# Moving weight splits, masks, loads and stores by a step in a two-batch encoder layer

## The chip, the cores and the metric

The kernel runs on one core of one Trainium2 chip. The metric is the device time of one execution in microseconds, as the median of several runs. The engines are TensorE (PE; its weight loads are shown as PEld), VectorE (DVE), ScalarE (ACT), GpSimd (POOL) and SyncE (SP), which only issues transfers here.

## What is computed

One layer of a bidirectional encoder is applied to two batches with shared weights: batch A (`x_prompt`, 1024 tokens) and batch B (`x_sample`, 512 tokens), 1024 channels each, all in fp32.

```python
h = rms_norm(x, pre_w)
cols = h @ w_in          # q|k, v, o, z, gates i and f; attention q, k, v, z; merge gates
y_m = mlstm_mixer(...)   # bidirectional mLSTM, 4 heads x 256, chunks of 128, forward and backward
y_a = dilated_attention(...) * silu(a_z)   # 3 (window, dilation) groups x 8 heads x 64
merged = sigmoid(g0) * (y_m @ w_pm) + sigmoid(g1) * (y_a @ w_pa)
out = merged @ w_out
return x + rms_norm(out, post_w)
```

Inside a chunk the mLSTM weighs the products of q and k with exp(d_log - m), which is zero on one side of the diagonal (on the other side for the backward direction); between chunks it carries a 256 x 256 state and its normaliser. The head's norm and the two gates follow.

## The kernel before

Every fp32 product is made of three matmuls on a pair of halves: `hi`, the operand rounded by a ScalarE copy, and `lo`, the rest by a subtraction on VectorE or GpSimd; `mm3` (line 191) multiplies hi x hi, hi x lo and lo x hi.

The kernel has two parts. The first, up to about 1055 us, makes all projections of batch A, and the value projections of both. The second makes everything else. In the second part TensorE and SP run in the order of the program text (line 1957), while the order on ScalarE, VectorE and GpSimd is chosen when the kernel is built, by a scheduler that models each instruction's time (line 2096). Every engine's queue is worked off in order. `issue_after(x)` orders the instructions of a block behind `x` on the same engine and adds no wait.

The second part is a row of five stages: mLSTM of A (`mlstm`, line 856), attention of A (`attend`, line 1431), mLSTM of B (`mlstm_short`), attention of B, and the rest. Each stage's work is short and full of dependences, so it is filled with dense products, one list for the whole part: the projections of batch B (`short_units`), the output projections of the three blocks of 512 tokens (`branches`, line 1627) and the last product with its norm (`final`, line 1692). A `Fill` object (line 113) hands them out: a unit takes eight steps, one step is the three matmuls of one slice of 128 channels (in `final`, of one slice and 128 tokens), and a stage calls `fill(share)`; `STEPS` and the stage's number of shares say how many steps a share is.

A unit's weights come by a transfer into one of two raw buffers (`load_w`) and are split into one of three pairs of halves (`split_w`, line 245), by ScalarE and VectorE; the very first low half is made on GpSimd. `weights()` (line 138), called by a unit at its first step, calls `load()` (line 124), which splits up to two units' weights at once, until two units are ahead (`ahead`, four from line 2021 on, with five pairs of halves), or as many as buffers are free. The transfer of the next raw weights is asked for behind each split, and issued at the next `tick()`, or at the split that needs it.

`tick()` (line 212) is called once a round. It issues `pace` of the queued loads (`spread(r)` sets the pace such that the queue is empty after `r` rounds) and the stores whose time has come: `put` holds a store back for `lag` rounds. `need(group)` issues what is still missing of a group.

In `mlstm` the rounds go over head, chunk and direction, 64 in all. `rows` loads, for two chunks, the rows of the stabiliser, broadcast to all partitions. `front(k + 1)`, written ahead of `core(k)`, makes the mask `rm` (line 923: an affine_select on GpSimd; line 925: an Exp on ScalarE), multiplies it with the products (line 926), splits the result into `sch` and `scl` (lines 929, 930) and makes the weighted q and k. `core` multiplies by the values into the PSUM tile `num`, of which there are two; line 989 (and 992 for the second half of the chunks) evicts it. `ml_load` (line 830) queues a head's q, k and v; the v tiles' last two columns are set by memsets on GpSimd (lines 846, 849), and head 1 uses other tiles (`V1a`, `V1b`) than head 0. Before the first stage `short_input` (line 651) splits the normalised input of batch B into the tiles `H`, the low halves of the first four slices by GpSimd (line 326); `aside` is the last of these.

In `mlstm_short`, `turn` transposes the normalised output (`hn`, line 1195) on TensorE (line 1202). In `attend` a round makes logits (line 1386), softmax (1398 to 1402), transposes of the weights (1409) and the output (1421), which is evicted at line 1423 into one of ten (A) or six (B) `ot` buffers and stored. `split` (line 1587) is a generator that runs beside dense units, brings rows of `ym` back, and splits them (lines 1604, 1605). `close`, in `final`, squares and sums a product (line 1709), and with the second half of the channels makes the norm and writes the result.

Of the kernel before, what the change touches and what calls it, by code (L numbers as in the profile page):

```python
# [112 lines left out]
class Fill:  # L113
# [3 lines left out]
    def __init__(self, net, units):  # L117
        self.net, self.units, self.gen = net, list(units), None
        self.srcs = [x for u in self.units for x in u.srcs]
        self.raws, self.ready, self.taken, self.base, self.ahead = [], [], 0, 0, 2  # L120
        self.rate = self.due = 0.0
        self.done = 0

    def load(self):

        more = 2
        while (len(self.ready) < min(self.base + len(self.net.wsplit), self.taken + self.ahead, len(self.srcs))
               and (more or len(self.ready) < self.taken)):
            more -= 1
            self.fetch(len(self.ready) + 1)  # L130
            self.ready.append(self.net.split_w(*self.raws[len(self.ready)]))
            self.fetch(len(self.ready) + 1)
# [5 lines left out]
    def weights(self, first=True):  # L138
# [4 lines left out]
        self.load()  # L143
# [11 lines left out]
    def step(self):  # L155
        while self.gen is not None or self.units:
            if self.gen is None:
                self.gen = self.units.pop(0).make(self.weights)
            if next(self.gen, self) is not self:
                self.done += 1  # L160
                return True
# [14 lines left out]
class Net:  # L176
# [653 lines left out]
    def ml_load(self, T, h):  # L830
# [12 lines left out]
        for i, x in enumerate([both[0][:, :1032], both[0][:, 1032:]] if S == BLK else both):  # L843
            x = x.rearrange("p (n c) -> p n c", c=258)
            if i:
                nc.gpsimd.memset(x[:, :, 256:258].bitcast(F32), 0.0)
            else:
                for c in range(2):
                    nc.gpsimd.memset(x[:, :, 256 + c:257 + c].bitcast(F32), 1.0 - 2 * c)
# [6 lines left out]
    def mlstm(self, T, fill, steps, first, banks, lead, after, beside=()):  # L856
# [7 lines left out]
        head, made, turns, rws = {0: first}, {}, {}, {}  # L864
        beside = iter(beside)
        self.lag = 2 if n > 4 else 3
        with ExitStack() as stack:
# [44 lines left out]

            def front(k):
# [5 lines left out]
                uc, wsc, flc = (T.col[:, q, o:o + 1] for q in range(3))  # L919
                rw = rws[h, d, c // 2 * 2][:, c % 2]  # L920
                rm = sb.tile([P, P], F32, name="rm")
                sg = 1 if d == 0 else -1
                nc.gpsimd.affine_select(out=rm, in_=rw[:, 0], pattern=[[sg, P]], compare_op=OP.is_ge, fill=-NEG, base=0,
                                        channel_multiplier=-sg)
                nc.scalar.activation(rm, rm, AF.Exp, scale=-1.0, bias=uc)
# [94 lines left out]
            for _ in prepare(0):  # L1020
                fill(1 / 3)
            front(0)
            coming = None
            for k, (h, i, d) in enumerate(rounds):
# [12 lines left out]
                if k % 4 < 2:  # L1037
                    rows(k // 4 + 1, k % 4)
                if k + 1 < len(rounds):
# [63 lines left out]
    def mlstm_short(self, T, fill, steps, first, banks, lead, after, beside=()):  # L1103
# [11 lines left out]
        with ExitStack() as stack:  # L1115
# [103 lines left out]
            for k, (h, i) in enumerate(rounds):  # L1219
# [20 lines left out]
                self.tick()  # L1240
                turns.pop(k - 1, lambda: None)()
                fill(2 / 3)
# [188 lines left out]
    def attend(self, T, fill, steps, first, banks, outs, after=None, beside=None, at=()):  # L1431
# [4 lines left out]
        self.lag = 3  # L1436
        with ExitStack() as st:
# [26 lines left out]
            for i in range(12):  # L1464
                now = coming
                for j, t in enumerate(now):
                    if j == 1:
                        if i < 11:
                            coming = ready(i + 1)
                            self.spread(T.n - 1 if i else 1)  # L1470
# [116 lines left out]
    def split(self, T, b, row, places, halves):  # L1587
# [5 lines left out]
        got = []  # L1593
        for j, (hi, lo) in enumerate(halves):
            for k in range(5):
                if k < 4:
                    r = row + 4 * j + k
                    t = self.rows_in.pop(0)
                    self.rows_in.append(t)
                    got.append(t)  # L1600
                    self.fetch(("ym", T.S, min(r // 2, 4)), t, T.ym[r, :, b * BLK:(b + 1) * BLK])
                if k:
                    t = got.pop(0)
                    nc.scalar.activation(hi[:, k - 1], t, AF.Copy)
                    nc.gpsimd.tensor_sub(lo[:, k - 1], t, hi[:, k - 1].bitcast(F32))
                yield
# [85 lines left out]
    def final(self, T, b):  # L1692
# [4 lines left out]
        def make(weights):  # L1697
# [8 lines left out]
            def close(u, t, c, p):  # L1706
                r0 = b * BLK + t * P
                o1 = sb.tile([P, BLK], F32, name="mg", bufs=2) if u else o[t]
                nc.scalar.activation(o1, p, AF.Square, accum_out=ss[:, t, u:u + 1])
                if u == 0:  # L1710
                    nc.vector.tensor_mul(o[t], p, pw[:, c])
                    return
                which, xt = xo[t]
                nc.vector.tensor_add(ss[:, t, 4:5], ss[:, t, 0:1], ss[:, t, 1:2])
                nc.gpsimd.tensor_scalar(ss[:, t, 5:6], ss[:, t, 4:5], 1.0 / D, 4 * EPS, op0=OP.mult, op1=OP.add)
# [43 lines left out]
def body(tc, a):  # L1759
# [3 lines left out]
    with ExitStack() as st:  # L1763
# [192 lines left out]
        with ExitStack() as s1:  # L1956
# [36 lines left out]
            with ExitStack() as s2:  # L1993
# [4 lines left out]
                with tc.issue_after(N.aside.ins):  # L1998
                    head = N.ml_load(A, 0)
# [100 lines left out]
```

## Time and profile before

| what | value |
|---|---|
| runs, us | 2284.59, 2285.61, 2280.73 (median 2284.59) |
| the profiled execution, us | 2280.13 |
| its span, us | 2278.3 |
| mean granted TensorE clock | 0.995 |
| PE / PEld busy | 98% / 86% |
| DVE / ACT / POOL busy | 65% / 48% / 27% |
| bytes moved | 425.05 MB, mean 187 GB/s |

The span runs from the first to the last instruction of the program. An engine's busy share is that of its own instructions, without the time in which it waits or issues transfers; the ends of matmuls are modelled. In a timeline a row is: start, duration, engine (with a q: its sequencer, as for transfers), line, operation, out<-in, shape, number, and in brackets the idle time before it and what ended that. In a table of waits the columns are the total, the number and the longest, in us. The granted clock is the share of TensorE's full clock that the throttle let through.

### The profile page before, as it was taken

The numbers are of one execution on the slowest core, as the hardware profiler recorded it, in microseconds if no ns is written. First come the engines' busy times: TensorE is split into PE (matmuls) and PEld (weight loads), VectorE is DVE, ScalarE is ACT, GpSimd is POOL, SyncE is SP. The second block draws the span as 40 slices with busy tenths as digits, with TensorE's granted clock in tenths as the row PEclk, the third lists the DMA queues.
The fourth block names the chain that finished last, engine by engine and source line by source line (L and its number), as shares of the span: only waits on it lengthen the run. The fifth ranks groups of instructions, "written<-read, shape, count | busy, mean of one in ns | idle before, by whom it ended". The sixth has DMA issues, their size and how long they took to land. (4 is left out here: it accounts for less than half of the span.)

```text
span 2278.3 us, 35138 instructions
## 1 busy us (share of the span) xinstructions
PE 2235.8 (98%) x12210; PEld 1950.2 (86%) x12210; DVE 1472.1 (65%) x2789; ACT 1103.1 (48%) x2255; POOL 615.6 (27%) x789
## 2 busy tenths in 40 slices
PE   9999999999999999999999999999999999999998
PEld 9999998888887888887888888989888888888787
DVE  5587556767889655544788775575567744555563
ACT  7444223434444433334777766676644444544432
POOL 1000023333333322222667640001033321411311
PEclk9999999999999999999999999999999999999999
DMA  9545335555323223324766659997777878787673
GB/s 361 188 138 145 112 113 193 197 194 194 126 102 111 93 83 114 136 93 159 250 210 223 159 160 232 237 243 205 207 238 253 258 232 243 207 252 212 225 246 115
DMA packets 253626, 425.05 MB, mean 187 GB/s; under 512 B 26208, under 2 KB 150752, under 8 KB 252680
## 3 DMA queue, kind: packets, MB, share of 16 engines
q1 hardware_dynamic: 249848, 410.20, 57.8%
q10 hardware_dynamic: 3600, 12.59, 1.4%
q8 instruction: 97, 1.59, 0.3%
q14 instruction: 81, 0.66, 0.1%
HBM read 302.72 MB, written 128.37 MB: 189 GB/s over the span
## 5 line engine op out<-in xcount | busy, mean ns | idle before, releaser
L194 PE MATMUL dense<-H,wh 128*128 128x512 f32 x672 | 282.1, 420 | 0.0
L195 PE MATMUL dense<-H,wh 128*128 128x512 f32 x672 | 265.9, 396 | 5.1 <-POOL H L326 5.0
L196 PE MATMUL dense<-H,wl 128*128 128x512 f32 x672 | 266.4, 396 | 0.2 <-DVE wl L253 0.2
L196 PE MATMUL d<-Hh,phla 128*128 128x512 f32 x608 | 236.9, 390 | 1.5 <-DVE phla L538 1.5
L195 PE MATMUL d<-Hl,phla 128*128 128x512 f32 x608 | 236.6, 389 | 0.0
L194 PE MATMUL d<-Hh,phla 128*128 128x512 f32 x608 | 236.5, 389 | 0.0
L195 PE MATMUL d<-vlo,Hh 128*128 128x322 f32 x704 | 219.7, 312 | 0.8 <-DVE vlo L384 0.8
L196 PE MATMUL d<-vhi,Hl 128*128 128x322 f32 x704 | 219.9, 312 | 0.0
L194 PE MATMUL d<-vhi,Hh 128*128 128x322 f32 x704 | 219.8, 312 | 0.0
L253 DVE TENSOR_TENSOR wl<-wraw,wh 128x1024 fp32r<-128x1024 f32 x109 | 139.2, 1277 | 85.3 <-ACT wh L252 83.3
L1398 DVE CUSTOM_DVE_ANT_0 ls<-lg,bias 128x256 f32<-128x256 f32 (+1 forms) x288 | 93.8, 362 | 146.6 <-PE lg L1386 61.7
L194 PE MATMUL d<-Hh,phlb 128*128 128x512 f32 x456 | 177.4, 389 | 0.0
L195 PE MATMUL d<-Hl,phlb 128*128 128x512 f32 x456 | 177.4, 389 | 0.0
L196 PE MATMUL d<-Hh,phlb 128*128 128x512 f32 x456 | 177.4, 389 | 0.0
L556 POOL TENSOR_TENSOR psum_w<-pw_raw 128x512 f32<-128x512 f32 x38 | 57.2, 1506 | 444.3 <-DMA pw_raw<-w_in 432.0
L1402 ACT ACTIVATE ls<-ls,nm 128x256 f32<-128x256 f32 (+1 forms) x288 | 130.5, 455 | 92.7 <-DVE nm L1400 78.7
L252 ACT ACTIVATE wh<-wraw 128x1024 fp32r<-128x1024 f32 x110 | 116.1, 1055 | 88.4 <-PE dense L195 34.4
L196 PEld LDWEIGHTS dense<-H,wl 128*128 128x128 f32 x672 | 127.3, 189 | 29.6 <-DVE wl L253 0.6
L195 PEld LDWEIGHTS dense<-H,wh 128*128 128x128 f32 x672 | 128.3, 191 | 20.8 <-POOL H L326 7.4
L194 PEld LDWEIGHTS dense<-H,wh 128*128 128x128 f32 x672 | 127.7, 190 | 13.6
L196 PEld LDWEIGHTS d<-Hh,phla 128*128 128x128 f32 x608 | 114.1, 188 | 26.4 <-DVE phla L538 2.8
L195 PEld LDWEIGHTS d<-Hl,phla 128*128 128x128 f32 x608 | 114.1, 188 | 23.9
(556 smaller groups left out, 5729.7 us busy)
## 6 DMA issues: line engine op xcount, KB each, us to landing
pw_raw<-w_in SPq DMA_DIRECT2D x76, 512.0 KB
wraw<-w_in SPq DMA_DIRECT2D x76, 512.0 KB
aqk_a<-pwk SPq DMA_DIRECT2D x48, 512.0 KB
aqk_b<-sw SPq DMA_DIRECT2D x48, 256.0 KB
wraw<-w_pm SPq DMA_DIRECT2D x24, 512.0 KB
wraw<-w_out SPq DMA_DIRECT2D x24, 512.0 KB
vb<-w_vp SPq DMA_DIRECT2D x16, 644.0 KB
va<-w_vp SPq DMA_DIRECT2D x14, 644.0 KB
```

The costliest lines, as they stand in the source:

```text
L194: nc.tensor.matmul(out, lh, rh, start=start, stop=False)
L195: nc.tensor.matmul(out, lh, rl, start=False, stop=False)
L196: nc.tensor.matmul(out, ll, rh, start=False, stop=stop)
L252: self.splits = (nc.scalar.activation(hi[:, :n], raw[:, :n], AF.Copy), on.tensor_sub(lo[:, :n], raw[:, :n], hi[:, :n].bitcast(F32)))
L253: on.tensor_sub(lo[:, :n], raw[:, :n], hi[:, :n].bitcast(F32)))
L556: self.nc.gpsimd.tensor_add(s[:, 0], ws[1][:, 0], ws[1][:, 1])
L1398: nc.vector.tensor_tensor_reduce(out=ls[:, hh], in0=ts["lg"][hh], in1=bt[:, hh], scale=1.0, scalar=NEG, op0=OP.add, op1=OP.max, accum_out= ...
L1402: nc.scalar.activation(ls[:, hh], ls[:, hh], AF.Exp, bias=nm[:, hh:hh + 1], accum_out=ot[:, 128 + hh:129 + hh])
```

## The change

- **Weights.** `weights()` splits only what the unit and its successor still lack; all further splits are made by `load()` after the unit's fourth step (`left` counts down). The initial `load()` and `release()` stay.
- **Memsets.** Every memset of the v tiles in `ml_load` is ordered behind `aside`; before, only those of head 0 of batch A were, with the whole call.
- **Masks.** The mask of a round is made by a function of its own, called for round k + 2 ahead of `front(k + 1)`; `rm` gets a third buffer.
- **`mlstm_short`.** `fill(2/3)` stands ahead of `turn` instead of behind it.
- **`attend`.** The loads of the second unit are spread over n - 1 rounds instead of one, and the lag of stores is 2 for batch B instead of 3.
- **`split`.** Rows of `ym` are asked for three steps ahead instead of one, across the two halves, with five buffers instead of three.
- **`close`.** The sum of squares is scaled in the square; the first half's sum gets its epsilon on GpSimd early, so that the addition on VectorE goes.

```diff
-        self.done = 0
+        self.done = self.left = 0
     def load(self):
...
-            self.fetch(len(self.ready) + 1)
-            self.ready.append(self.net.split_w(*self.raws[len(self.ready)]))
-            self.fetch(len(self.ready) + 1)
+            self.split()
+    def split(self):
+        self.fetch(len(self.ready) + 1)
+        self.ready.append(self.net.split_w(*self.raws[len(self.ready)]))
+        self.fetch(len(self.ready) + 1)
     def fetch(self, n):
...
-        self.load()
+        room = min(self.base + len(self.net.wsplit), len(self.srcs))
+        while len(self.ready) < max(self.taken, min(self.taken + 1, room)):
+            self.split()
+        self.left = 4
     def release(self):
...
+                self.left -= 1
+                if self.left == 0:
+                    self.load()
...
-            if i:
-                nc.gpsimd.memset(x[:, :, 256:258].bitcast(F32), 0.0)
-            else:
-                for c in range(2):
-                    nc.gpsimd.memset(x[:, :, 256 + c:257 + c].bitcast(F32), 1.0 - 2 * c)
+            with self.tc.issue_after(self.aside.ins):
+                if i:
+                    nc.gpsimd.memset(x[:, :, 256:258].bitcast(F32), 0.0)
+                else:
+                    for c in range(2):
+                        nc.gpsimd.memset(x[:, :, 256 + c:257 + c].bitcast(F32), 1.0 - 2 * c)
...
-        head, made, turns, rws = {0: first}, {}, {}, {}
+        head, made, turns, rws, masks = {0: first}, {}, {}, {}, {}
...
+            def mask(k):
+                h, i, d = rounds[k]
+                c = i if d == 0 else n - 1 - i
+                o = 32 * d + h * n + c
+                uc = T.col[:, 0, o:o + 1]
+                rw = rws[h, d, c // 2 * 2][:, c % 2]
+                rm = sb.tile([P, P], F32, name="rm", bufs=3)
+                sg = 1 if d == 0 else -1
+                nc.gpsimd.affine_select(out=rm, in_=rw[:, 0], pattern=[[sg, P]], compare_op=OP.is_ge, fill=-NEG, base=0,
+                                        channel_multiplier=-sg)
+                nc.scalar.activation(rm, rm, AF.Exp, scale=-1.0, bias=uc)
+                masks[k] = rw, rm
             def front(k):
-                uc, wsc, flc = (T.col[:, q, o:o + 1] for q in range(3))
-                rw = rws[h, d, c // 2 * 2][:, c % 2]
-                rm = sb.tile([P, P], F32, name="rm")
-                sg = 1 if d == 0 else -1
-                nc.gpsimd.affine_select(out=rm, in_=rw[:, 0], pattern=[[sg, P]], compare_op=OP.is_ge, fill=-NEG, base=0,
-                                        channel_multiplier=-sg)
-                nc.scalar.activation(rm, rm, AF.Exp, scale=-1.0, bias=uc)
+                wsc, flc = (T.col[:, q, o:o + 1] for q in (1, 2))
+                rw, rm = masks.pop(k)
...
+            mask(0)
             front(0)
+            mask(1)
                 self.tick()
...
                     rows(k // 4 + 1, k % 4)
+                if k + 2 < len(rounds):
+                    mask(k + 2)
                     front(k + 1)
...
                 self.tick()
+                fill(2 / 3)
-                fill(2 / 3)
...
-        self.lag = 3
+        self.lag = 3 if T.n > 4 else 2
...
                         if i < 11:
-                            self.spread(T.n - 1 if i else 1)
+                            self.spread(T.n - 1)
...
-        got = []
-        for j, (hi, lo) in enumerate(halves):
-            for k in range(5):
-                if k < 4:
-                    r = row + 4 * j + k
-                    t = self.rows_in.pop(0)
-                    self.rows_in.append(t)
-                    got.append(t)
-                    self.fetch(("ym", T.S, min(r // 2, 4)), t, T.ym[r, :, b * BLK:(b + 1) * BLK])
-                if k:
-                    t = got.pop(0)
-                    nc.scalar.activation(hi[:, k - 1], t, AF.Copy)
-                    nc.gpsimd.tensor_sub(lo[:, k - 1], t, hi[:, k - 1].bitcast(F32))
-                yield
+        got, m = [], 4 * len(halves)
+        for i in range(m + 3):
+            if i < m:
+                t = self.rows_in.pop(0)
+                self.rows_in.append(t)
+                got.append(t)
+                self.fetch(("ym", T.S, min((row + i) // 2, 4)), t, T.ym[row + i, :, b * BLK:(b + 1) * BLK])
+            if i >= 3:
+                t, (hi, lo), k = got.pop(0), halves[(i - 3) // 4], (i - 3) % 4
+                nc.scalar.activation(hi[:, k], t, AF.Copy)
+                nc.gpsimd.tensor_sub(lo[:, k], t, hi[:, k].bitcast(F32))
+            yield
     def along(self, units, make, every):
...
             def close(u, t, c, p):
-                nc.scalar.activation(o1, p, AF.Square, accum_out=ss[:, t, u:u + 1])
+                nc.scalar.activation(o1, p, AF.Square, scale=1.0 / 32, accum_out=ss[:, t, u:u + 1])
+                    nc.gpsimd.tensor_scalar(ss[:, t, 4:5], ss[:, t, 0:1], 4 * EPS, None, op0=OP.add)
                 which, xt = xo[t]
-                nc.vector.tensor_add(ss[:, t, 4:5], ss[:, t, 0:1], ss[:, t, 1:2])
-                nc.gpsimd.tensor_scalar(ss[:, t, 5:6], ss[:, t, 4:5], 1.0 / D, 4 * EPS, op0=OP.mult, op1=OP.add)
+                nc.gpsimd.tensor_scalar(ss[:, t, 5:6], ss[:, t, 1:2], ss[:, t, 4:5], None, op0=OP.add)
...
-                with tc.issue_after(N.aside.ins):
-                    head = N.ml_load(A, 0)
+                head = N.ml_load(A, 0)
...
-            N.rows_in = [N.sraw[:, :BLK]] + [N.osb.tile([P, BLK], F32, name=f"ymr{i}") for i in range(2)]
+            N.rows_in = [N.sraw[:, :BLK]] + [N.osb.tile([P, BLK], F32, name=f"ymr{i}") for i in range(4)]
```

## The prediction

> **What bounds the kernel now.** I read the page first, then a table of busy time by stage, then TensorE's own waits, and at last the timelines of the engines around each long gap.
>
> ```profile
> span 2278.3 us, 35138 instructions
> ...
> PE 2235.8 (98%) x12210; PEld 1950.2 (86%) x12210; DVE 1472.1 (65%) x2789; ACT 1103.1 (48%) x2255; POOL 615.6 (27%) x789
> ```
>
> TensorE is the bound: 2235.8 of 2278.3 us. The change adds and removes no matmul, so all it can return is idle time, 42.5 us, and time at a lowered clock. The profiled execution took 2280.13 us, 1.83 more than its span and 4.5 below the median of 2284.59; I sum against the execution and take the difference from the median. In the stage table the columns are stretch, PE busy, PEld, DVE, ACT, POOL, granted clock, DMA share, GB/s.
>
> ```profile
> 1054.70:1071.00 16.30, 11.24 (x35) 7.42 (x34) 10.89 (x8) 2.97 (x6) 11.99 (x17) 0.79 0.88 300
> 1071.00:1100.00 29.00, 25.96 (x159) 22.02 (x158) 17.22 (x37) 19.60 (x45) 12.00 (x19) 1.00 0.82 287
> 1100.00:1345.00 245.00, 238.32 (x1509) 212.44 (x1508) 194.99 (x423) 179.39 (x452) 171.95 (x289) 0.99 0.60 194
> 1345.00:1385.00 40.00, 34.91 (x204) 29.75 (x203) 21.40 (x65) 20.22 (x55) 3.12 (x12) 0.96 0.72 183
> ...
> 1660.00:1835.00 175.00, 171.13 (x1018) 149.75 (x1017) 128.34 (x308) 76.70 (x145) 55.50 (x89) 1.00 0.80 250
> 1835.00:1900.00 65.00, 60.88 (x315) 51.49 (x314) 29.48 (x65) 31.62 (x72) 19.70 (x18) 0.95 0.88 267
> 1900.00:2130.00 230.00, 228.52 (x1215) 194.49 (x1215) 120.33 (x313) 109.61 (x304) 56.07 (x53) 1.00 0.73 210
> 2130.00:2272.00 142.00, 140.90 (x618) 113.88 (x616) 81.30 (x137) 42.85 (x67) 23.89 (x28) 1.00 0.64 214
> ```
>
> Stretch less PE busy is idle; one less the clock, times the stretch, is what the slow clock costs. Idle plus clock by stage: start of the second half (1054.7 to 1071) 5.1 + 3.4; first mLSTM rounds 3.0; the other rounds 6.7 + 2.4; start of attention A 5.1 + 1.6; short mLSTM 3.9; start of attention B 4.1 + 3.3; its rest 1.5; end 1.1. With the tail behind the last matmul that is most of the idle time, and nothing of the change lies before 1054.7. TensorE's waits (total, times, longest) name what it waits for:
>
> ```profile
> PE num L194 <- ACT X L989: 6.4, 6, 2.3
> PE pt L1409 <- ACT ls L1402: 6.3, 4, 3.7
> PE o L1421 <- ACT ot L1423: 5.5, 3, 2.9
> PE dense L195 <- POOL H L326: 5.0, 2, 4.4
> PE a L1202 <- ACT hn L1195: 2.4, 2, 1.4
> ```
>
> Four of five end on ScalarE, which is only 48% busy: it was blocked in order behind an instruction that waited for something else.
>
> **Start of the second half (V1 memsets behind `aside`, third split later).**
>
> ```profile
> 1042.62 1.06 ACT L252 ACTIVATE wh<-wraw 128x1024 fp32r<-128x1024 f32 x1 [3.34 <-DMA wraw<-w_in]
> 1045.08 4.27 ACT L325 ACTIVATE H<-xs 128x512 fp32r<-128x512 f32 x8
> 1054.79 0.15 POOL L849 MEMSET V1a<- 128x8 f32 x2 [20.41 <-PE d L195]
> 1054.93 2.35 POOL L253 TENSOR_TENSOR wl<-wraw,wh 128x1024 fp32r<-128x1024 f32 x1
> 1057.24 7.30 POOL L326 TENSOR_TENSOR H<-xs,H 128x512 fp32r<-128x512 f32 x4
> 1058.29 6.80 DVE L326 TENSOR_TENSOR H<-xs,H 128x512 fp32r<-128x512 f32 x4
> 1059.54 0.50 PE L195 MATMUL dense<-H,wh 128*128 128x512 f32 x1 [4.36 <-POOL H L326]
> 1070.45 0.39 PE L194 MATMUL dense<-H,wh 128*128 128x512 f32 x1
> 1071.13 0.39 PE L891 MATMUL a<-Q,K 128*128 128x128 f32 x2
> ...
> SPq L231 <- DMA K<-qk_a: 4.2, 2, 2.4
> 1067.03 0.36 SPq L231 DMA_DIRECT2D V0b<-vs_a  x1
> ```
>
> GpSimd's queue is headed by the memset of V1a, whose place the last product of the first half frees only at 1054.79. Behind it stand the first low half (2.35 us) and four pieces of the input (7.30), whose sources ScalarE had written by 1043.7 and from 1045.6 on. With the memsets behind `aside` GpSimd can start at 1043.7 and, at the same durations, ends by 1053.4: before TensorE asks. So the 4.36 us gap goes. VectorE's four pieces, at their old 1.7 us each from about 1057 on, may still hold single steps, but end by 1064, and that matters to nobody, since what is late next is K. The lead of 4 shares is 4 x 210 / 74 = 11 dense steps of 0.68 us (1071.13 less 1070.45), 7.5 us: TensorE is through them at 1062.3 and then needs K, whose second half SP saw land at 1067.03 (it issued V0b on that). So the first product of Q and K comes at 1067.0 instead of 1071.1: 4.1 us gained, but behind a new gap of 4.7 us, and a slow clock after it; the stages with gaps of 3.7 and 2.9 us (the waits above) paid 1.6 and 3.3 for theirs, I take 2.6. Net 1.5. In the first rounds I give back half of the 3.0 us idle, since one wait for a buffer fewer stands before SP's row loads: 1.5. Together 3.0, between -1 (the masks want their rows a round sooner just here, where the transfers are busiest) and 8.
>
> On that clock: the Trainium skill, "TensorE: Matmul & The Clock Gate", Part 1, lets the array fall to half rate only after at least one idle window of about 3.4 us. Here the stage whose longest gap is 2.9 us fell to 0.95, so the trace has it earlier, and the trace decides. By the page's rule the clock in that stage and in the mLSTM rounds would owe nothing to those gaps, and the sum below would be some 5 us smaller.
>
> **mLSTM rounds (masks a round ahead).** Added: one tile; no instruction. Moved: per round one affine_select on GpSimd and one Exp on ScalarE, each ahead of the front of the round before.
>
> ```profile
> 1285.78 1.32 POOL L923 TENSOR_SCALAR_AFFINE_SELECT rm<-rw 128x128 f32<-128x128 f32 x1
> 1287.13 0.40 ACT L925 ACTIVATE rm<-rm,col 128x128 f32<-128x128 f32 x1 [1.98 <-POOL rm L923]
> 1288.44 0.39 PE L194 MATMUL num<-V1a,sch 128*128 128x258 f32 x1 [2.33 <-ACT X L989]
> ...
> L923 POOL TENSOR_SCALAR_AFFINE_SELECT rm<-rw x64: 286/294/1321, 1067.7 to 1330.5; 128x128 f32<-128x128 f32 x64
> ...
>   DMA rw<-rw_a: 10.0, 6
> ...
>   ACT rm L925: 37.6, 38
> ...
> 1083.69 0.42 SPq L231 DMA_DIRECT2D rw<-rw_a  x1
> 1089.49 0.29 POOL L923 TENSOR_SCALAR_AFFINE_SELECT rm<-rw 128x128 f32<-128x128 f32 x1 [2.41 <-DMA rw<-rw_a]
> ```
>
> The longest gap of the rounds is this chain: the mask took 1.32 us instead of its median 0.29, ScalarE waited 1.98 for it, and the eviction L989 that frees `num` stood behind. A mask that was made a round (4.2 us: 262.8 / 63) before cannot hold ScalarE there. This gap and its clock go: 2.3 + 1.6 = 3.9 (the stage's rounded clock says 2.4; 1.6 is what the longer gap of attention A cost). The other 4.4 us of gaps I leave. Against it: ScalarE waited 37.6 us in all for masks, while the stage lost 8.3 us (6.7 + 1.6), 0.22 us per us; the same ratio prices the rows, which now have two rounds (8.4 us) from issue to use instead of three, and needed 5.8 at 1083.69. Behind a mask that waits stand `qw`, `scl` and `ql` on GpSimd, and on ScalarE the evictions. Bounds -4 to 7.
>
> **Weights in the middle of a unit.**
>
> ```profile
> L253 DVE TENSOR_TENSOR wl<-wraw,wh 128x1024 fp32r<-128x1024 f32 x109 | 139.2, 1277 | 85.3 <-ACT wh L252 83.3
> ```
>
> Counts stay; a split of 1.06 us on ScalarE and 1.28 on VectorE moves by four steps. ScalarE no longer waits for the last matmul of the unit before, whose buffer it takes. The weights are still due 12 steps, 8.2 us of pure dense work, after their split. No row gives this a price on TensorE: 0, with the bounds in the 5 us of new gaps below. At the closing projections, where four units are ahead, as many splits fall due per unit as before.
>
> **Start of attention A (`spread`).**
>
> ```profile
> 1368.81 0.33 SPq L210 DMA_DIRECT2D wraw<-w_in  x1
> ...
> 1378.34 1.06 ACT L252 ACTIVATE wh<-wraw 128x1024 fp32r<-128x1024 f32 x1 [8.64 <-DMA wraw<-w_in]
> ```
>
> All loads of the second unit are issued in one round; the raw weights behind them go out at 1368.81 and land at 1378.3, 9.5 us later, with ScalarE standing at their split for 8.64. That makes the 3.7 us wait of the transposes and the slow clock after it, 3.7 + 1.6. Over seven rounds it is two loads a round, as for every later unit. I take 5.3 and allow 3.5 to 6.5.
>
> **Short mLSTM (`fill(2/3)` ahead of `turn`).** Two thirds of a share are 164 / 36 x 2/3 = 3 steps, 2.1 us of cover where the waits were 1.4 and 1.0: 2.4 gone. Without that cover they are back. The transposed result is stored 2 us later, which nobody waits for. Bounds 0 and 2.5.
>
> **Attention B (`lag` 2, rows of `ym` three ahead, `spread`).**
>
> ```profile
> 1873.23 0.63 ACT L1604 ACTIVATE K<-ymr 128x512 fp32r<-128x512 f32 x1 [1.19 <-DMA ymr<-ym_a]
> 1886.61 0.42 DVE L1398 CUSTOM_DVE_ANT_0 ls<-lg,bias 128x256 f32<-128x256 f32 x1 [3.93 <-DMA og_b<-ot]
> ```
>
> VectorE waited 3.93 us for the store of an `ot` buffer, and TensorE's longest wait on an eviction L1423, 2.9 us, came behind it. A round holds six dense steps (290 / 48), 4.1 us, beside its own products, so a store issued one round earlier has landed by then. SP then waits at that store for its eviction L1423, and the loads behind it wait with it, but the eviction is a full round old. The other two of the three waits on L1423 (2.6 of 5.5 us) stand behind ScalarE's waits for a row of `ym`, 1.19 in the one shown; three rows ahead remove them, one at this start and one in the 1.5 us idle after 1900. I take 6.5 of 7.4, and 1.0. Bounds 3 to 9.
>
> **The closing sums.** Twelve VectorE additions leave the chain, twelve GpSimd ones come beside the first half, on an engine that is busy for 24 of 142 us there; the last addition stood on the end of the kernel:
>
> ```profile
> 2272.76 0.16 DVE L1714 TENSOR_TENSOR ss<-ss 128x1 f32<-128x1 f32 x1 [1.65 <-ACT mg L1709]
> ```
>
> 0.2 there, and 0.5 of the 1.1 idle before.
>
> **Sum.** 3.0 + 3.9 + 5.3 + 2.4 + 6.5 + 1.0 + 0.7 = 22.8. ScalarE's, VectorE's and GpSimd's orders are chosen anew by the scheduler's own model; for what that puts in a wrong place I charge 5, some five gaps of the size of those on `num` (6.4 in 6). Gain 18: 2262 for a profiled execution, 2266.6 for the median.
>
> **Rivals.** *Gaps move instead of vanishing*: DMA share is 0.88 in both start stages, so raw weights, rows and stores stay late and only mask, turn and closing sums pay: 3.9 + 2.4 + 0.7 less 2 = 5, 2279.6. For it: K at 1067 already limits the first term. Against: between 1900 and 2130 the share is 0.73 with 1.5 us idle. *The change doesn't do what it says*: the scheduler orders by modelled readiness, so the masks and splits may stand where they stood; then only program-ordered TensorE and SP edits (spread, lag, turn) count, against new gaps: 2284 give or take 5. *Rows too late, slower*: in the rounds each of the 30 row loads holds GpSimd and, behind it, ScalarE. At 3.1 us a row that is 93 us x 0.22 = 20.5 lost, against 14 gained elsewhere: 2291. It decides from 2.1 us a row, which is a row landing 10.5 us after issue; for it, SP issued the first rows late; against, the 5.8 us above and only six waits, 10.0 us, in before.
>
> **How the numbers follow.** Forecast 0.66, gaps move 0.17, not as it says 0.10, rows late 0.07. About 0.2%, 4.6 us, is what can be told from no change here. Faster by more: 0.66 + 0.12 + 0.04 = 0.82; within: 0.05 + 0.04 = 0.09; slower: 0.07 + 0.02 = 0.09. The forecast's own range is a gain of 10 to 27 us, half way to the sums of the terms' ends (about 1.5 and 35): 2257.6 to 2274.6; reaching into the second and third case, and leaving out the slow one, 2254 to 2281.
>
> **What would show it.** Right: the first dense unit runs from 1054.8 without a wait for POOL H, then a gap of about 4 to 5 us before L891; no ACT rm wait on POOL above 1 us late in the rounds; no wait of ScalarE above 4 us for raw weights near the start of attention A; no VectorE wait for og_b; no wait before L1202. PE busy stays near 2236 less the clock's share. Wrong: GpSimd waiting for rw many times over, gaps on `num` as before, or a new wait for `wl` at the head of dense units.

## The result, and the profile after

The changed kernel takes 2306.43 us (median of 4 runs, 2300.89 to 2311.26) where the kernel before takes 2284.02 (median of 4, 2280.73 to 2285.61): a ratio of 1.0101, 95% interval 1.0083 to 1.0119. It is slower by some 22 us; 18 us faster was forecast. The profiled execution took 2300.89 us, its span is 2299.1.

The page of the changed kernel, where only line numbers have moved (by 9 to 23):

```profile
span 2299.1 us, 35128 instructions
...
PE 2243.4 (98%) x12210; PEld 1956.4 (85%) x12210; DVE 1466.8 (64%) x2777; ACT 1098.9 (48%) x2255; POOL 622.6 (27%) x801
```

The same 12210 matmuls are busy 7.6 us longer (2243.4 less 2235.8), mostly because they ran at half clock more often: TensorE was busy for 32.1 us of half clock, before for 19.6, and half of the difference is 6.2 us. The rest of the 20.8 us between the two spans, 13.2 us, is new idle time. To see where, one looks up when TensorE passes the same instruction in both traces. The group of the output products of attention A, first in the kernel before and then in the changed one (columns: shortest, median and longest in ns, first and last start in us):

```profile
L1421 PE MATMUL o<-K,pts x640: 217/275/422, 1361.3 to 1657.2; 128*128 128x64 f32 x160
```

```profile
L1444 PE MATMUL o<-K,pts x640: 216/275/421, 1367.0 to 1671.6; 128*128 128x64 f32 x160
```

Their last start is 14.4 us late. The same look at other places gives this table, in us against the profile of before (minus is earlier); the lower rows are experiments that are told below:

| kernel | first Q x K | first `num` | last `num`, mLSTM A | last `o`, attention A | last transpose, short mLSTM | last `o`, attention B | end |
|---|---|---|---|---|---|---|---|
| changed | -6.9 | -1.7 | +3.3 | +14.4 | +14.3 | +18.2 | +20.8 |
| weights alone | -1.9 | -1.9 | -2.4 | +15.5 | +20.4 | +17.4 | +18.7 |
| changed, weights undone | -7.3 | -2.8 | +2.0 | +0.7 | -2.1 | +0.7 | +3.4 |
| changed, early request | -7.6 | -2.9 | +1.7 | -2.4 | -3.8 | -0.6 | +0.5 |
| masks alone | -1.9 | -1.9 | +6.0 | +6.6 | +7.6 | +5.7 | +6.8 |
| picked edits | -6.5 | -2.4 | -1.5 | -6.4 | -9.1 | -11.7 | -8.0 |

Each figure comes from one execution. The kernel with the masks alone has no edit behind the rounds, and its later stages still differ from before by 0.7 to 1.9 us, so that a difference of two us in one stage is not told from chance here.

Attention A alone loses 11.1 us: 5.7 are idle time of TensorE, and 5.1 come from the clock, which is halved four times there instead of once. Nothing of the change but `spread` and the weights touches it. What ScalarE waited for there, in the kernel before and in the changed one (total, times, longest):

```profile
ACT wh L252 <- DMA wraw<-w_in: 9.3, 2, 8.6
```

```profile
ACT wh L261 <- DMA wraw<-w_in: 31.4, 14, 5.7
```

The one wait of 8.6 us that the prediction named is gone, and fourteen stand in the place of two. TensorE's own waits in attention A, changed kernel:

```profile
PE pt L1432 <- ACT ls L1425: 6.3, 6, 2.1
PE o L1444 <- ACT pts L1435: 5.0, 2, 3.3
PE lg L1409 <- DVE ot L1421: 1.4, 1, 1.4
```

Five of these nine, the longest of 3.33 us, one of 2.07 and three of about 0.5, 7.0 us together, end on ScalarE's softmax or eviction, which stood in its queue behind a split whose raw weights had landed late. Of the others, two at the start of the stage (2.1 us) stand there in the kernel before too (1.2 us); one of 1.89 us comes behind two ACT_TABLE_LOAD instructions of ScalarE, 1.28 us each, and one of 1.65 behind ScalarE's wait of 3.2 us for a store. The longest in full. First two neighbouring splits of the kernel before with the transfer between them, then of the changed kernel the same two splits, their transfer and the product that was held:

```profile
1466.20 1.05 ACT L252 ACTIVATE wh<-wraw 128x1024 fp32r<-128x1024 f32 x1
1466.79 0.34 SPq L210 DMA_DIRECT2D wraw<-w_in  x1
1478.02 1.04 ACT L252 ACTIVATE wh<-wraw 128x1024 fp32r<-128x1024 f32 x1
```

```profile
1476.24 1.06 ACT L261 ACTIVATE wh<-wraw 128x1024 fp32r<-128x1024 f32 x1 [4.90 <-DMA wraw<-w_in]
1482.21 0.43 SPq L219 DMA_DIRECT2D wraw<-w_in  x1
1491.33 1.06 ACT L261 ACTIVATE wh<-wraw 128x1024 fp32r<-128x1024 f32 x1 [5.66 <-DMA wraw<-w_in]
1492.92 0.60 ACT L1435 ACTIVATE pts<-pt 128x512 f32<-128x512 f32 x1
1493.57 1.11 PE L1444 MATMUL o<-K,pts 128*128 128x64 f32 x8 [3.33 <-ACT pts L1435]
```

Before, the transfer goes out 0.6 us after the earlier split, lands 9.5 us later, and the split that needs it starts with no wait. Changed, it goes out 6.0 us after the earlier split, ScalarE stands 5.66 us at the next one, the eviction `pts` stands behind it, and TensorE waits 3.33 us.

Over the 28 splits of attention A, from the trace: the median from issue to landing is 5.0 us in both, so the transfers are as fast as they were. The median from issue to the start of the split is 11.0 us before and 5.8 after. Splits that start within 0.3 us of the landing: 2 before, 18 after. And the split itself has hardly moved: counted in dense matmuls that ran before it (24 to a unit), it stands 0 to 3 matmuls behind the end of a unit in 26 of 28 cases before and in 22 of 28 after, although the text of the changed kernel puts it 12 matmuls in.

### The profile page after: what moved, and what is told of

Its sections match the earlier page's. It is cut to its first block, busy times and chain, and to the rows that moved or that the text cites. A ratio compares the mean times of both kernels' runs of the same rounds, so it can differ in the third digit from the quotient of the medians.

```text
span 2299.1 us, 35128 instructions
## 1 busy us (share of the span) xinstructions
PE 2243.4 (98%) x12210; PEld 1956.4 (85%) x12210; DVE 1466.8 (64%) x2777; ACT 1098.9 (48%) x2255; POOL 622.6 (27%) x801
## 5 line engine op out<-in xcount | busy, mean ns | idle before, releaser
L203 PEld LDWEIGHTS d<-vhi,Hh 128*128 128x128 f32 x704 | 133.4, 190 | 1.2 <-issue 0.8
```

The costliest lines, as they stand in the source:

```text
L203: nc.tensor.matmul(out, lh, rh, start=start, stop=False)
```

## The theory and its rivals

Theory, **late transfers**: the scheduler that orders ScalarE put the splits back to the end of the unit before, where their buffer becomes free; the transfer of the next raw weights, asked for behind the split in the text, is issued by SP, which keeps the order of the text, half a unit later than it was. Rivals: the loss in attention A is that of the spread loads; or a split in the middle of a unit costs by itself (three pairs of halves, a new order on ScalarE). Apart from it: the masks, and the two places where attention B and the closing stage got slower instead of faster.

## The experiments

Twelve kernels, with the kernel before on the same chip each time (its medians there: 2278.94, 2280.72 and 2280.17 us). The ratios are taken over all the runs and can differ by 0.1% from the quotients of these medians. Stage times are from the profiled execution of each kernel.

**1. Weights alone**, on the kernel before:

```diff
-        self.load()
+        room = min(self.base + len(self.net.wsplit), len(self.srcs))
+        while len(self.ready) < max(self.taken, min(self.taken + 1, room)):
+            self.split()
+        self.left = 4
...
+                self.left -= 1
+                if self.left == 0:
+                    self.load()
```

> Kernel before with the weights' edit alone (third and later splits asked for after the unit's fourth step). Theory (late transfers): on ScalarE the split stays at the end of a unit, where the scheduler had it, but its transfer is issued half a unit later by SP, which keeps program order; the lead from issue to split in attention A falls from a median of 11 us to about 6 while a transfer takes 5, ScalarE stands over 20 us there for raw weights (9.3 before), and the kernel is slower than before by 8 to 14 us, 2292 to 2298. Rival (the loss in attention A is that of the spread loads): no wait of this kind, 2284 give or take 3.

Measured: 2305.00 us against 2278.94, ratio 1.01, interval 1.0083 to 1.0118. Attention A takes 17.9 us longer, and ScalarE's waits for raw weights there are

```profile
ACT wh L261 <- DMA wraw<-w_in: 41.3, 13, 10.9
```

The sign and the place are the theory's; the size, 26 us in the medians and 18.7 in the profiled execution, is above the 8 to 14 expected. The spread loads are not the cause, since this kernel does not have them.

**2. The changed kernel with the weights undone** (the hunks of 1 reversed).

> Changed kernel with the weights' edit undone, all other edits kept. Theory (late transfers): attention A gets back the 11 us that it lost and some of the 5 that spread was to bring, 2290 to 2296 beside 2306 of the changed kernel; ScalarE's waits for raw weights in attention A fall below 8 us. Rival (spread): stays at 2302 to 2310.

Measured: 2281.91, below the expected 2290 to 2296; ratio to before 1.0014, interval 1.0004 to 1.0025. Attention A is 1.4 us shorter than before. Undoing the weights' edit takes back 20 of the 22 us; but all the other edits together, forecast to gain 23 us less 5 for new gaps, bring no gain.

**3. The changed kernel with the transfer asked for at the unit's start**, the split left in the middle:

```diff
+        self.fetch(len(self.ready) + 2)
         self.left = 4
```

> Changed kernel with one line more: at the unit's start the transfer of the next but one raw weights is asked for, as early as in the kernel before, while the split is still written in the middle of the unit. Theory (late transfers): lead back at about 11 us, waits for raw weights gone, 2290 to 2297, like the kernel with the weights' edit undone. Rival (the place of the split itself, three pairs of halves and a new order on ScalarE): stays at 2302 or more.

Measured: 2282.44, ratio 1.0017, interval 1.0006 to 1.0028, like kernel 2 and better than expected. The lead is back at 10.6 us, and ScalarE waits 2.3 us in two places. The place of the split in the text, the number of halves and their buffers are those of the changed kernel: only the time of the request differs. This shows the cause.

**4. Spread in attention A only**, in the changed kernel:

```diff
-                            self.spread(T.n - 1)
+                            self.spread(T.n - 1 if i or T.n > 4 else 1)
```

> Changed kernel with the loads of the second unit spread over all rounds in attention A only; in attention B they go out in one round as before. Theory (spread in B is too late): in B a unit has four rounds, the last two loads go out in the round that needs them, which makes the 5.0 us gap at the start of attention B; it goes with half of the slow clock behind it: 2306 less 5 to 8, 2298 to 2301. Rival (the loads are late because SP stands behind raw weights and rows of ym): 2304 to 2308.

What it is about is TensorE's first long wait in attention B of the changed kernel, and the last loads of that unit on SP:

```profile
1875.59 1.09 SPq L240 DMA_DIRECT2D V1a<-aqk_b  x2
```

```profile
1881.57 1.12 PE L1409 MATMUL lg<-V1a,Q 128*128 128x256 f32 x2 [5.03 <-DMA sraw<-ym_a]
```

(The wait is put down to the transfer that came last; the two loads of `V1a`, which the product reads, landed at 1881.48 and 1882.07.) Measured: the wait is gone, and attention B is 3.2 us shorter than in the changed kernel; but the time is 2308.93, ratio 1.0134, interval 1.0115 to 1.0153: the expected 5 to 8 us do not show. These four runs lie between 2298 and 2315, which covers a few us. The mechanism is shown in the profile, its worth is not.

**5. The picked edits**: the kernel before with memsets, spread in attention A, turn, `lag` 2 and rows of `ym` three ahead; weights, masks, closing sums and spread in attention B left out.

> Kernel before with the edits that look harmless: memsets behind aside, spread in attention A only, turn behind two thirds of a share, lag 2, rows of ym three ahead. Left out: weights, masks, closing sums, spread in attention B. Theory (each of these gives what its stage showed in the kernel with the weights' edit undone): start 2.8, attention A 1.4 to 4, short mLSTM 1.4 to 2.7, attention B 3 to 6 without the new gap: 9 to 14 us below the kernel before of the same runs. Rival (what one stage gives the next takes back, since the transfers do not come earlier): within 4 us of the kernel before.

Measured: 2272.87 against 2280.72, ratio 0.9969, interval 0.9959 to 0.998. It beats both kernels, the one before by 7.9 us, a little below the expected 9 to 14: the stages gave 2.4 (start), 5.0 (attention A), 2.6 (short mLSTM) and 2.6 (attention B), 12.6 together; 1.0 of it is lost again in the rounds, and 3.7 in the closing stage, which this kernel computes as before.

```profile
PE dense L194 <- DVE mg L1716: 3.5, 2, 2.0
```

There VectorE runs the combination of the attention groups (six multiplications of 0.68 us and additions, waiting for loads of `og_b`) ahead of the multiplication that frees TensorE's accumulator. This order came with edits in other stages; it was not tried to undo it.

**6. Masks alone**, on the kernel before.

> Kernel before with the masks' edit alone. Theory (rows late): the scheduler leaves most masks next to their use, and those that it puts early stand in front of rows that have not landed; GpSimd's waits for rows grow from 9.5 us in five to over 15 us, and the rounds lose 3 to 6 us: 2 to 6 us slower than before. Rival (the rounds lose because they begin 3 us earlier while the transfers do not): masks alone cost nothing, within 2 us. Third (as predicted): 3 to 4 us faster, and no 2.3 us gap near 1286.

Measured: 2285.34 against 2280.72, ratio 1.0017, interval 1.0005 to 1.0029; the rounds are 7.8 us longer. GpSimd's waits for rows of the stabiliser over the rounds, before and with the masks alone:

```profile
POOL rm L923 <- DMA rw<-rw_a: 9.5, 5, 2.5
```

```profile
POOL rm L922 <- DMA rw<-rw_a: 20.2, 11, 4.1
```

The sign is the theory's, and the total lies in its range, while the rounds lose more than the 3 to 6 us expected. One part was wrong: the masks did move, from a median of 6.2 us to 9.7 us before the copy to `sch` that uses them. And the gap that the prediction wanted to remove is there unchanged:

```profile
1285.18 0.30 POOL L922 TENSOR_SCALAR_AFFINE_SELECT rm<-rw 128x128 f32<-128x128 f32 x1
1288.43 1.32 POOL L922 TENSOR_SCALAR_AFFINE_SELECT rm<-rw 128x128 f32<-128x128 f32 x1
```

```profile
1289.78 0.40 ACT L924 ACTIVATE rm<-rm,col 128x128 f32<-128x128 f32 x1 [2.04 <-POOL rm L922]
1290.57 0.46 ACT L998 ACTIVATE X<-num,r 128x256 f32<-128x256 f32 x1
```

```profile
1291.09 0.39 PE L194 MATMUL num<-V1a,sch 128*128 128x258 f32 x1 [2.33 <-ACT X L998]
```

Counted from the first round, the mask of 1.32 us in the kernel before is that of round 52, and the product it holds is that of round 50. With the masks a round ahead, round 52's mask takes 0.30 us, and now the mask of round 53 stands in the same place, takes 1.32 us, and holds the same product of round 50 for the same 2.33 us. What stands in that place on VectorE is the low half of a weights' split, in the kernel before and with the masks alone:

```profile
1285.73 1.21 DVE L253 TENSOR_TENSOR wl<-wraw,wh 128x1024 fp32r<-128x1024 f32 x1
```

```profile
1288.38 1.22 DVE L253 TENSOR_TENSOR wl<-wraw,wh 128x1024 fp32r<-128x1024 f32 x1
```

Over all 14 traces 78 masks of this stage took more than 0.8 us where the median is 0.29. Of these, 76 began while VectorE made such a low half and ended 0.15 us behind it. So a mask is long when it begins behind a running `wl`, and masks that are made earlier change which of them does so: seven in the kernel before, five with the masks alone.

**7. The picked edits and the weights with the early request.**

> The picked kernel and the weights' edit with the transfer asked for at the unit's start as in the kernel before. Theory (the split stays where it was, so moving it in the text is worth nothing once its transfer is early): within 2 us of the picked kernel. Rival (a split in the middle of a unit frees ScalarE): 2 to 6 us faster than the picked kernel.

Measured: 2275.41 against 2280.72, ratio 0.9982, interval 0.9969 to 0.9994, beside 0.9959 to 0.998 of the picked kernel. No gain from the split's place, as the theory has it; by the medians it is 2.5 us behind the picked kernel, where 2 was the bound expected.

**8 and 12. The dose**: the changed kernel with the later splits asked for after the second or the sixth step.

```diff
-        self.left = 4
+        self.left = 2
```

> Changed kernel with the later splits asked for after the unit's second step instead of its fourth. Theory (late transfers): a step in attention A takes 290 or so over 202, 1.4 to 1.5 us, so the lead falls by 3 us from 11 to about 8, still above the 5 us of a transfer; few waits are left and most of the 24 us goes: 2284 to 2291 where the changed kernel takes 2306. Rival (any split that is not at the unit's start costs the same): above 2299.

> Changed kernel with the later splits asked for after the unit's sixth step instead of its fourth. Theory (late transfers): the lead, 11 us at the unit's start and about 6 at step 4 with the waits in it, goes below the 5 us of a transfer, each of the 28 splits in attention A waits about 3 us more unless it is itself moved back; 15 to 40 us slower than the changed kernel, 2320 to 2345. Rival (a fixed cost of every split that is not at the start): as the changed kernel, 2300 to 2310.

Measured: 2281.34 (ratio 1.0003, interval 0.9992 to 1.0013) and 2327.69 (1.0199, 1.0175 to 1.0224). ScalarE's waits for raw weights in attention A at step 2, and at step 6:

```profile
ACT wh L261 <- DMA wraw<-w_in: 5.0, 3, 2.4
```

```profile
ACT wh L261 <- DMA wraw<-w_in: 61.1, 18, 6.2
```

| request | lead, us (median) | waits there, us | ratio to before |
|---|---|---|---|
| unit's start (kernel 3) | 10.6 | 2.3 | 1.0017 |
| step 2 | 10.1 | 5.0 | 1.0003 |
| step 4 (the change) | 5.8 | 31.4 | 1.0101 |
| step 6 | 5.8, waits included | 61.1 | 1.0199 |

It is no fixed price for a split off the unit's start: nothing up to step 2, where the lead fell by 0.5 us and not by the 3 expected, and from there some 22 us for each two steps, with a lead near the 5 us of a transfer.

**9. The picked edits and the masks, with the rows a round earlier:**

```diff
-            rw_of = Rot(self, [sb.tile([P, BLK], F32, name=f"rw{i}", bufs=1) for i in range(4)])
+            rw_of = Rot(self, [sb.tile([P, BLK], F32, name=f"rw{i}", bufs=1) for i in range(6)])
...
-                if k % 4 < 2:
-                    rows(k // 4 + 1, k % 4)
+                if (k + 1) % 4 < 2:
+                    rows((k + 1) // 4 + 1, (k + 1) % 4)
```

> The picked kernel and the masks' edit, with the rows of the stabiliser asked for one round earlier into six buffers instead of four, so that a row has as many rounds to its mask as in the kernel before. Theory (rows late): GpSimd's waits for rows fall back below 10 us, the rounds take what they take in the picked kernel, total within 2 us of it (2272.9 beside 2280.7 before, 7.8 faster). Rival (the new order on GpSimd costs by itself): 3 to 8 us slower than the picked kernel.

Measured: 2274.98 against 2280.17, ratio 0.9969, interval 0.9955 to 0.9983, the ratio of the picked kernel. The rounds are as long as before (+0.2 us), and the waits for rows are

```profile
POOL rm L923 <- DMA rw<-rw_a: 12.7, 4, 7.9
```

of which 7.9 is the first, at the start of the stage, which the picked kernel has too. With the rows earlier the loss of the rounds is gone, as the theory has it, and the masks ahead are worth nothing even so. The sum of these waits does not set the loss alone, though: kernel 11, told below, has the masks of before and 27.7 us of these waits (8.2 in the first), and its rounds are as long as before.

**10. As 9, with every mask ordered ahead of the front of the round before it** on GpSimd and ScalarE:

```diff
-                    front(k + 1)
+                    with self.tc.issue_after(a.ins), self.tc.issue_after(b.ins):
+                        front(k + 1)
```

> As the run before, and in each round the instructions of the front are ordered on GpSimd and ScalarE behind the next round's mask, so that every mask really is made a round ahead. Theory of the prediction (a mask made a round before cannot hold ScalarE, and the gap near 1286 goes): no wait of ScalarE for a mask over 1 us late in the rounds, 2 to 4 us faster than the picked kernel. Rival (GpSimd is a quarter busier beside VectorE than its own 0.29 us says, and the front only moves back): gap there, same or slower than the picked kernel by up to 6 us.

Measured: 2275.40, ratio 0.9972, interval 0.9959 to 0.9985. No gain over the picked kernel. Near 1283 TensorE still waits 1.42 us for an eviction L1000, less than the 2.33 of before; ahead of that eviction ScalarE waited 0.72 us for a mask and then made a weights' split of 1.04. The rounds are 2.2 us longer than before, so the forecast gain does not come even with the order enforced.

**11. The picked edits with the raw weights asked for one unit earlier:**

```diff
             self.ready.append(self.net.split_w(*self.raws[len(self.ready)]))
-            self.fetch(len(self.ready) + 1)
+            self.fetch(len(self.ready) + 2)
```

> The picked kernel with the raw weights asked for one unit earlier: behind a split the transfer for the split after the next is asked for, into the buffer just split. Theory (the transfer's lead is what counts, and 11 us is enough for most): ScalarE's last waits for raw weights go, 0 to 4 us faster than the picked kernel. Rival (SP stands at the buffer until VectorE has made the low half, and all loads behind it are late): 3 us slower or more.

Measured: 2279.42 against 2280.17, ratio 0.9998, interval 0.9983 to 1.0013: it gives the gain back. The lead is 20 us and no split of attention A waits for its transfer, but SP now stands at the buffer until VectorE has made the low half; in attention B, picked kernel and this one:

```profile
SPq L210 <- DVE wl L253: 7.7, 4, 2.5
```

```profile
SPq L210 <- DVE wl L253: 25.0, 8, 4.8
```

Attention B loses 3.5 us there against before, where the picked kernel gains 2.6. This is what the rival said, but SP's waits at its stores, for the eviction of `ot`, fell at the same time, picked kernel and this one:

```profile
SPq L210 <- ACT ot L1424: 39.5, 17, 5.0
```

```profile
SPq L210 <- ACT ot L1424: 14.3, 8, 3.5
```

So no run shows that SP's waits made the loss; that a request may also be too early is a possible reading.

## Why the prediction was wrong

**Weights.** The step that failed is "Counts stay; a split of 1.06 us on ScalarE and 1.28 on VectorE moves by four steps ... 0, with the bounds in the 5 us of new gaps below". It asked when the halves are due (8.2 us of dense work later) and not when the raw weights land. Behind each split the text asks for the next raw weights. The trace of before had what was needed: 11 us of lead, 5 of transfer, and splits 11.8 us apart (1466.20 to 1478.02 above), so that half a unit later, 6 us, leaves no more than a transfer. The price was not 0. Measured: 26 us slower alone (kernel 1); undone in the changed kernel, the ratio falls from 1.0101 to 1.0014, 20 us (kernel 2). The second rival came nearest in its mechanism, "the masks and splits may stand where they stood; then only program-ordered TensorE and SP edits (spread, lag, turn) count", but it counted the raw weights' transfer among the splits, not among SP's edits.

**Masks.** "A mask that was made a round (4.2 us: 262.8 / 63) before cannot hold ScalarE there" failed. The mask that stood there was that of a round two ahead, so it was early already; what cost was its place in front of an eviction, and that it met VectorE's low half `wl`. Forecast a gain of 3.9, measured 4.6 us slower alone. The slow rival named the right wait (rows), but its price per us of waiting does not hold as a constant: 10.7 us more of GpSimd's waits went with 7.8 us of the rounds in kernel 6, 0.7 us per us and not 0.22; within the rounds, 14.7 more went with 4.9 in the changed kernel, and 12.4 more with nothing in kernel 11.

**Start of the second half.** The path was right: the wait for the input's low halves is gone, TensorE is through the lead at 1062.3, and then it waits for K, 3.7 us where 4.7 was forecast:

```profile
1062.31 0.39 PE L205 MATMUL dense<-H,wl 128*128 128x512 f32 x1
1064.25 0.49 PE L901 MATMUL a<-Q,K 128*128 128x128 f32 x2 [1.56 <-DMA K<-qk_a]
1066.85 0.35 PE L901 MATMUL a<-Q,K 128*128 128x128 f32 x1 [2.12 <-DMA K<-qk_a]
```

Up to the first `num` that is 2.4 to 2.9 us in kernels 2, 3 and 5 against 3.0 forecast, and 1.7 in the changed kernel. But kernels 1 and 6, which do not have this edit, pass there 1.9 us earlier than the profile of before as well, so that the size of the gain is not shown.

**Spread.** For attention A near the forecast of 5.3 in some kernels, 5.0 us (kernel 5) and 4.0 (kernel 3), and less in others that have it, 1.4 (kernel 2) and 2.7 (kernel 9); with the weights late nothing of it could be seen. For attention B the prediction gave `spread` no term: there a unit has only four rounds, so the last two loads of the second unit go out just when they are needed, a wait of 4.9 to 6.4 us in kernels 2, 3 and 8 too.

**Short mLSTM.** Within its bounds or close: 2.6 us in kernel 5, 2.7 in kernel 2, 1.4 in kernel 3, 0.2 in kernel 11, against 2.4.

**Attention B.** Forecast 7.5, measured 2.6 in kernel 5; kernel 6, without any of these edits, is 1.9 us shorter there too, so that hardly a gain is shown. VectorE's waits for the stores of `ot` fell from 18.7 us to 7.2 there, as `lag` 2 was to do; but ScalarE's waits for rows of `ym` rose from 21.6 to 31.0, and TensorE's longest wait on the eviction is still 2.4 us.

**Closing.** Forecast 0.7, measured 1.2 to 3.7 us lost in kernels 2, 3, 5 and 7, with and without the closing sums; kernels 1 and 6 lose 1.3 and 1.1 as well. So it is not the sums: in kernel 5, TensorE's waits behind VectorE's new order are 3.0 of the 3.7 us. What sets that order stays open.

**New gaps.** The 5 us charged for the scheduler's new orders are near what the rounds (1.0) and the closing stage (3.7) lose in kernel 5; they were no bound for an edit that shifts a transfer.

**The clock.** It cost more than the idle time shows: 7.6 us of longer matmuls beside 13.2 of idle. The Trainium skill, "TensorE: Matmul & The Clock Gate", Part 1, has the array fall to half rate after an idle window of about 3.4 us; here no gap of attention A was longer than 3.33 us. One stretch of the changed kernel, behind a gap of 2.07 us at 1409 (columns as in the stage table):

```profile
1412.80:1416.10 3.30, 3.30 (x14) 3.01 (x13) 3.06 (x9) 2.01 (x7) 0.10 (x1) 0.50 0.00 0
```

The trace does not agree with the length: a gap of 2.07 us was enough here.

## What to carry to other kernels

When a step is moved in the text, list what it issues, and for each transfer the lead from issue to use and its duration; in a kernel where a scheduler orders the engines but the transfers keep the order of the text, the step may not move at all and its transfer will. A lead can be cut for free while it stays well above the duration of the transfer (10 us against 5 here); where it comes down to that duration (5.8 us here), an engine that works in order stands, with all that is queued behind it. A wait on an engine's queue is not cured by making the waiting instruction earlier, as long as another of its kind takes its place: ask which round it belonged to, and what made it long.

## What the runs showed of the hardware

**GpSimd and VectorE side by side.** The four low halves of the input that each makes, in the kernel before, where they run at the same time:

```profile
L326 POOL TENSOR_TENSOR H<-xs,H x4: 1712/1730/2245, 1057.2 to 1062.8; 128x512 fp32r<-128x512 f32 x4
L326 DVE TENSOR_TENSOR H<-xs,H x4: 1744/1760/1768, 1058.3 to 1063.3; 128x512 fp32r<-128x512 f32 x4
```

and in the changed kernel, where GpSimd is done before VectorE begins:

```profile
L335 POOL TENSOR_TENSOR H<-xs,H x4: 1295/1298/1302, 1046.7 to 1050.4; 128x512 fp32r<-128x512 f32 x4
L335 DVE TENSOR_TENSOR H<-xs,H x4: 683/683/684, 1057.0 to 1058.8; 128x512 fp32r<-128x512 f32 x4
```

VectorE takes 0.68 us instead of 1.76, GpSimd 1.30 instead of 1.73. The prediction kept 1.7 us for VectorE. The Trainium skill, "SBUF — State Buffer", section "Who interferes with whom", says that a VectorE instruction with two SBUF inputs contends with a GpSimd one that reads SBUF. The trace agrees: side by side, one of each takes about 1.75 us, more than either takes in the changed kernel and a little under their sum, 0.68 + 1.30.

**The clock and where a gap lies.** Kernels 9 and 10 have nearly the same two gaps at the start of the short mLSTM, 0.5 and 1.1 us in kernel 9, 0.7 and 1.1 in kernel 10. In kernel 10 the clock is halved for the next 3.4 us, in kernel 9 it is not. Kernel 10, then kernel 9:

```profile
1663.00:1666.40 3.40, 1.64 (x8) 1.00 (x7) 3.35 (x7) 2.14 (x4) 1.91 (x2) 1.00 1.04 352
1666.40:1669.80 3.40, 3.40 (x10) 2.62 (x9) 3.26 (x7) 1.06 (x1) 1.14 (x1) 0.50 0.99 283
```

```profile
1661.70:1665.10 3.40, 2.87 (x14) 1.98 (x13) 3.39 (x10) 2.68 (x6) 1.07 (x2) 1.00 1.07 316
1665.10:1668.50 3.40, 2.36 (x11) 2.00 (x12) 3.23 (x6) 1.10 (x2) 2.51 (x2) 1.00 0.94 269
```

The stretches are cut on the grid of the trace's own record of the granted clock: within each of the 14 traces, half-clock stretches begin whole multiples of 3.413 us apart. In kernel 10 both gaps fall into one such window, and TensorE is busy for 1.64 of its 3.4 us; in kernel 9 they fall into two, with 2.87 and 2.36 us busy. Of the 78 half-clock stretches in the 14 traces, 75 follow a window in which TensorE was busy for less than half (the other three 52 to 69%), and each of the 64 windows under 45% is followed by half clock. So a gap of one to two us may cost 1.7 us more or nothing, by where it falls in the window, and the sum over many such gaps is what an estimate can carry.
